# Splits, loads and norm steps around an MLP's products, put in another order

## The chip, the core and the metric

The kernel runs on one core of one Trainium2 chip. The time is device microseconds of one execution of the whole program on that core, and the figure that counts is the median over runs. In the views of the profile PE is TensorE (matmuls and transposes; PEld is its weight load), DVE is VectorE, ACT is ScalarE, POOL is GpSimd and SP is SyncE, which here only issues DMA transfers; POOL issues DMA transfers too. "L72" is line 72 of the kernel. Each engine works through its own instructions in a fixed order, and that order is settled when the program is built.

## The reference

A small decoder of two layers over 512 tokens and a width of 1024. Layer 0 mixes tokens by gated linear attention, layer 1 by stick-breaking attention; each is followed by a post-LayerNorm, an MLP of width 4096 and another post-LayerNorm:

```python
def layer_norm(x, g, b):
    xf = x.astype(jnp.float32)
    mu = jnp.mean(xf, axis=-1, keepdims=True)
    var = jnp.mean(jnp.square(xf - mu), axis=-1, keepdims=True)
    y = (xf - mu) * lax.rsqrt(var + LN_EPS)
    return (y * g.astype(jnp.float32) + b.astype(jnp.float32)).astype(x.dtype)

def sq_relu_mlp(x, w_up, w_down):
    h = jax.nn.relu(x @ w_up)
    return (h * h) @ w_down

    for layer in range(DEPTH):
        ...
        h = layer_norm(DEEPNORM_ALPHA * h + mix, ln_g[layer, 0], ln_b[layer, 0])
        h = layer_norm(DEEPNORM_ALPHA * h + sq_relu_mlp(h, mlp_w_up[layer], mlp_w_down[layer]),
                       ln_g[layer, 1], ln_b[layer, 1])
```

Everything is in fp32. After MLP 0 the shared keys and values (`kv_w`) and the queries of layer 1 are computed.

## The kernel before

**Products.** An fp32 product is made of three matmuls: each operand is split into a high part (`hi`, a copy to fp32r on ACT) and a low part (`lo`, the difference, on DVE), and hi x hi, hi x lo and lo x hi are summed in PSUM. A weight piece of 256 x 512 (a tile of 128 x 1024, half a megabyte) is split by `split_tile` (L70 on ACT, L72 on DVE); an operand made from activations is split by `put` (L98 on ACT, L99 on DVE). The split pieces lie in two pools, tags `hi` and `lo`, of eight buffers each; weights that are split straight after their load come through `raw`, three buffers (`split_piece`, L64).

**Seven steps.** A product of 2 x 2 blocks is done as seven block products instead of eight, by sums of blocks. In the output projection of layer 0 these are `seven` (L348 on): its last three products are called p3, p7 and p4, each of two halves s of 12 matmuls (L402), and each half is added to a row tile of the residual stream (`add`, L167 and L169 on DVE). In the MLP they are the seven steps of `steps` (L835): `make_blocks` loads and splits the weights of a step, `make_operand` sums and splits its activations, `go` runs its matmuls and reads the banks. Some block sums are done by DMA: `Blocks.more` (L761) adds a second block onto a loaded one by an accumulating load on POOL's queue, and `sum` (L784, L786) adds two loaded blocks, on POOL's DMA queue or on DVE.

**The MLP.** `mlp` (L806) takes the width of 4096 in four chunks c; each chunk has seven up steps (`part` at L942, matmuls L951, 48 of 256 columns each) and seven down steps (`part` at L992, matmuls L998, 24 of 512 columns). `todo` is the list of all 56 steps. `run_all` (L1022) writes them in order: at step n it prepares step n + 2. At step 0 it prepares steps 0, 1 and 2. The first two steps of chunk 0 take unsummed weights, four pieces of `plain` (L981 to L984): in MLP 0 they are loaded there, in MLP 1 they are handed over in `up0`, loaded and split inside `project` (L1483 to L1492).

**The joints.** Four row tiles t of 128 tokens are normed one after the other as their last additions come in. `finish` (L284) does it: `stats` (two DVE statistics L177, their sum L182, then `ve` L183 and the power `rs` L184 on POOL) and `centre` (L192 on DVE); then `turn_affine` transposes the centred tile in two halves (L271 on PE) and applies gain and bias in four copies per half (L274 on ACT). Tiles 0 and 1 are turned first (their second halves in `seconds`, pinned); tiles 2 and 3 are kept back in the list `late`, which the up step's `part` works off between matmuls. At the end of an MLP, tiles 0 and 1 get their statistics by sums on ACT (`stats_apart`, L206: a sum L209, `less` L210 on DVE, the squares L211, `ve` L212 on DVE, the power L213 on POOL). In MLP 0 this joint leads into `values` (L1090, matmuls L1111), in MLP 1 into the output (`done1`).

**What sets the order.** A list scheduler orders each engine's instructions by priority, which is their order in the program text, as soon as it reckons their inputs ready; statistics and centring are marked as urgent (`tc.high_priority`). `keep`, which is `tc.keep_in_program_order`, pins an instruction behind everything written before it on its engine. DMA issues are instructions of the queue's engine, SP or POOL, and stand in the same order.

## Time and profile before

| what | us |
|---|---|
| median of 3 runs | 1111.3 (1111.24 to 1111.48) |
| the profiled execution | 1109.4 |
| its span, first to last instruction | 1107.7 |
| PE busy | 1083.0 (98%) |
| DVE busy | 901.0 (81%) |
| ACT busy | 673.9 (61%) |
| POOL busy | 170.6 (15%) |

The profiled execution is one of its own, 1.9 us shorter than the median; what lies between its span and its time, 1.7 us, is before the first and after the last instruction of the program. PE is nearly always busy, so most of what the other engines do lies beside matmuls and costs nothing; a row of DVE or ACT matters where PE waits for it. The views give for a group or an instruction its duration and, in brackets, how long its engine stood idle before it and which instruction ended that idle time.

### The profile page before, as it was taken

How to read it: one execution, taken by the hardware profiler on the slowest of the kernel's cores; microseconds unless marked ns; L12 is line 12 of the kernel's file. 1: busy time of each engine (PE TensorE's matmuls, PEld its weight loads, DVE VectorE, ACT ScalarE, POOL GpSimd, SP SyncE). 2: the span in 40 equal slices, each digit the busy share in tenths (PEclk: the TensorE clock that was granted, in tenths of full speed). 3: DMA queues.
4: the chain of work that ended last, by engine and by line, in shares of the span. 5: the costliest groups of instructions: out<-in, count | busy, mean ns of one | idle time of the engine just before them, and what ended most of it. 6: DMA issues, size and time to landing. Idle time of an engine off the chain costs nothing. (4 is left out here: it accounts for less than half of the span.)

```text
span 1107.7 us, 16724 instructions
## 1 busy us (share of the span) xinstructions
PE 1083.0 (98%) x6463; PEld 936.9 (85%) x6463; DVE 901.0 (81%) x1086; ACT 673.9 (61%) x973; POOL 170.6 (15%) x201
## 2 busy tenths in 40 slices
PE   9999999989999999999999999999999999999997
PEld 7888888788899898898688778788888998988985
DVE  4488646989988978877888987689899889788778
ACT  4455436487557466465784766684875565574664
POOL 1021130302102101101203001222111021011012
PEclk9999999999999999999999999999999999999999
DMA  7262395688859949958837524478678598499583
GB/s 222 76 175 70 118 246 157 163 233 207 240 143 233 232 139 234 242 136 195 222 81 190 134 96 114 95 150 248 174 185 253 136 245 229 137 225 243 148 217 76
DMA packets 121891, 195.43 MB, mean 176 GB/s; under 512 B 13978, under 2 KB 38938, under 8 KB 121812
## 3 DMA queue, kind: packets, MB, share of 16 engines
q1 hardware_dynamic: 94932, 136.16, 38.4%
q0 software_dynamic: 26592, 57.68, 29.3%
q8 instruction: 51, 0.84, 0.3%
q10 hardware_dynamic: 288, 0.52, 0.1%
q14 instruction: 28, 0.23, 0.1%
HBM read 176.52 MB, written 3.15 MB: 162 GB/s over the span
## 5 line engine op out<-in xcount | busy, mean ns | idle before, releaser
L72 DVE TENSOR_TENSOR lo<-B,hi 128x1024 fp32r<-128x1024 f32 x206 | 246.7, 1220 | 60.7 <-ACT hi L70 58.6
L70 ACT ACTIVATE hi<-B 128x1024 fp32r<-128x1024 f32 x206 | 212.3, 1054 | 123.3 <-DVE B L786 63.4
L998 PE MATMUL ps<-hi,T 128*128 128x512 f32 x896 | 280.4, 391 | 1.8 <-DVE T L99 1.5
L951 PE MATMUL ps<-T,hi 128*128 128x256 f32 x1280 | 233.9, 284 | 6.3 <-ACT T L98 4.1
L951 PEld LDWEIGHTS ps<-T,hi 128*128 128x128 f32 x1280 | 200.1, 192 | 10.3 <-ACT T L98 4.9
L998 PEld LDWEIGHTS ps<-hi,T 128*128 128x128 f32 x896 | 167.6, 188 | 38.8 <-DVE T L99 3.4
L951 PE MATMUL ps<-T,lo 128*128 128x256 f32 x640 | 179.9, 283 | 0.0
L998 PE MATMUL ps<-lo,T 128*128 128x512 f32 x448 | 174.9, 390 | 2.8 <-DVE lo L72 2.8
L951 PEld LDWEIGHTS ps<-T,lo 128*128 128x128 f32 x640 | 122.3, 192 | 0.3
L72 DVE TENSOR_TENSOR lo<-raw,hi 128x1024 fp32r<-128x1024 f32 x86 | 103.0, 1216 | 20.1 <-ACT hi L70 19.7
L70 ACT ACTIVATE hi<-raw 128x1024 fp32r<-128x1024 f32 x88 | 91.0, 1056 | 38.7 <-PE ps L94 9.4
L998 PEld LDWEIGHTS ps<-lo,T 128*128 128x128 f32 x448 | 84.2, 188 | 20.8 <-DVE lo L72 4.0
L951 PE MATMUL ps<-A,hi 128*128 128x256 f32 x512 | 92.5, 283 | 0.0
L93 PE MATMUL ps<-T,hi 128*128 128x512 f32 (+1 forms) x200 | 79.7, 399 | 0.4 <-DVE k L99 0.4
L951 PEld LDWEIGHTS ps<-A,hi 128*128 128x128 f32 x512 | 79.9, 192 | 0.0
L98 ACT ACTIVATE T<-s 128x1024 fp32r<-128x1024 f32 (+1 forms) x52 | 51.5, 993 | 43.7 <-DVE s L883 37.6
L761 POOL DMA_DIRECT2D B<-in_mlp_w_down_dram x32 | 38.3, 1198 | 257.5 <-DMA B<-in_mlp_w_down_dram 126.0
L94 PE MATMUL ps<-T,hi 128*128 128x512 f32 (+1 forms) x200 | 76.5, 383 | 0.1
L95 PE MATMUL ps<-T,lo 128*128 128x512 f32 (+1 forms) x200 | 76.5, 383 | 0.0
L169 DVE TENSOR_TENSOR h<-h,ps 128x512 f32<-128x512 f32 x108 | 70.9, 678 | 2.8 <-PE ps L998 2.8
L951 PE MATMUL ps<-A,lo 128*128 128x256 f32 x256 | 72.4, 283 | 0.0
L99 DVE TENSOR_TENSOR T<-s,T 128x1024 fp32r<-128x1024 f32 (+1 forms) x52 | 59.2, 1138 | 5.7 <-ACT T L98 5.7
(239 smaller groups left out, 1877.6 us busy)
## 6 DMA issues: line engine op xcount, KB each, us to landing
B<-in_mlp_w_up_dram SPq DMA_DIRECT2D x64, 512.0 KB, 5.2
B<-in_mlp_w_down_dram SPq DMA_DIRECT2D x64, 512.0 KB, 4.9
B<-in_mlp_w_up_dram POOLq DMA_DIRECT2D x32, 512.0 KB, 8.3
B<-in_mlp_w_down_dram POOLq DMA_DIRECT2D x32, 512.0 KB, 9.4
raw<-in_mlp_w_up_dram SPq DMA_DIRECT2D x24, 512.0 KB, 4.6
B<-B POOLq DMA_DIRECT2D x24, 512.0 KB, 5.8
raw<-in_gla_w_in_dram SPq DMA_DIRECT2D x20, 512.0 KB, 3.7
raw<-in_mlp_w_down_dram SPq DMA_DIRECT2D x16, 512.0 KB, 8.2
```

What stands on the lines that cost most here:

```text
L70: keep(nc.scalar.activation(hi, raw, AF.Copy))
L72: keep((on or nc.vector).tensor_tensor(lo, raw, hi.bitcast(F32), op=ALU.subtract))
L93: keep(nc.tensor.matmul(ps, lhsT=a[0], rhs=b[0], start=first, stop=False))
L94: keep(nc.tensor.matmul(ps, lhsT=a[0], rhs=b[1], start=False, stop=False))
L95: keep(nc.tensor.matmul(ps, lhsT=a[1], rhs=b[0], start=False, stop=last))
L98: keep(nc.scalar.activation(hi, ps, AF.Copy))
L99: keep((on or nc.vector).tensor_tensor(lo, ps, hi.bitcast(F32), op=ALU.subtract))
L169: nc.vector.tensor_tensor(h, h, ps, op=op)
L761: keep(nc.gpsimd.dma_start(out=got[h].rearrange("p (a b) -> p a b", a=2), in_=self.w(other[0], h, other[1]), accum_op=ALU.add))
L951: nc.tensor.matmul(to, lhsT=b[k][x][:, fs], rhs=a(k)[:, y], start=opens and f % 2 == 0 and (k, x, y) == (0, 0, LO), stop=closes and (k, x) ...
L998: nc.tensor.matmul(banks[s], lhsT=a(k)[:, x][:, P * s:P * s + P], rhs=b[k][y], start=opens and (k, x, y) == (0, LO, 0), stop=closes and (k ...
```

## The change

It adds and removes no matmul. Its parts, in the order of the kernel:

- In `seven`, the splits of p4 are written after the second addition of p3, pinned on ACT and DVE.
- In MLP 0, pieces 1 and 2 of the first weights are loaded through POOL's queue and not pinned; piece 3 stays pinned on SP. The accumulating loads onto block (1, 1) are issued by `late`, after a small POOL copy that reads tile 3's `rs` and pins them behind it.
- In both MLPs, the blocks of step 2 are written after the matmuls of step 0; tile 3 is turned in step 0 and no longer in step 1; steps 8 to 13 make their operand before their blocks; the matmuls of the first down step are pinned.
- In `project`, the last piece of the first weights of MLP 1 is loaded and split after the last addition, unpinned.
- `stats_apart` is cut in two. Tiles 0 and 1 both draw their sums first, then both their squares; `less` and `ve` are computed on ACT.

```diff
-    def split_piece(src, a, turn=lambda ins: ins, **how):
+    def split_piece(src, a, turn=lambda ins: ins, queue=nc.sync, **how):
...
-        turn(nc.sync.dma_start(out=raw.rearrange("p (a b) -> p a b", a=a), in_=src))
+        turn(queue.dma_start(out=raw.rearrange("p (a b) -> p a b", a=a), in_=src))
...
-            total, less, squares, ve, rs = (small(1, tag) for tag in ("total", "less", "squares", "ve", "rs"))
+            self.junk = junk
+            total, self.less = small(1, "total"), small(1, "less")
             nc.scalar.activation(junk, self.h, AF.Copy, accum_out=total)
-            nc.vector.tensor_scalar(less, total, -1.0 / D, None, op0=ALU.mult)
-            nc.scalar.activation(junk, self.h, AF.Square, bias=less, accum_out=squares)
-            nc.vector.tensor_scalar(ve, squares, 1.0 / D, LN_EPS, op0=ALU.mult, op1=ALU.add)
-            nc.gpsimd.tensor_tensor(rs, ve, mhalf[:, 0:1], op=ALU.pow)
-            self.less, self.rs = less, rs
+            nc.scalar.activation(self.less, total, AF.Copy, scale=-1.0 / D)
+
+        def power_apart(self):
+
+            squares, ve, self.rs = small(1, "squares"), small(1, "ve"), small(1, "rs")
+            nc.scalar.activation(self.junk, self.h, AF.Square, bias=self.less, accum_out=squares)
+            nc.scalar.activation(ve, squares, AF.Copy, scale=1.0 / D, bias=LN_EPS)
+            nc.gpsimd.tensor_tensor(self.rs, ve, mhalf[:, 0:1], op=ALU.pow)
...
                     hs[t].stats_apart(junk)
+                    if t == 1:
+                        for h in hs[:2]:
+                            h.power_apart()
+                            h.centre()
                 else:
                     hs[t].stats()
-                hs[t].centre()
+                    hs[t].centre()
...
-        p4 = split_a(a22), split_b(3)
         for s in range(2):
             part(s, *p3, zs, False, True)
             add(s, zs, 0, 1, last=True)
+            if s == 1:
+                p4 = split_a(a22, keep=tc.keep_in_program_order), split_b(3, keep=tc.keep_in_program_order)
             yield s
...
-                made.append(Blocks(mlp_, weights, AHEAD[2:] + AHEAD[:1], by))
+                made.append(Blocks(mlp_, weights, (AHEAD[2], (1, 1, None if late_sum else (0, 1)), AHEAD[0]), by))
...
+                    me.late = lambda: [made[0].more(made[0].b[1, 1], (0, 1), h, keep) for h in range(2)]
...
-                    if c == 0 and late and (n == 0 and m == 9 and len(late) > 1 or n == 1 and m == 1):
+                    if c == 0 and n == 0 and late and m in (9, 13):
                         late.pop(0)()
...
-                    plain = [piece(0)] + [lambda k=k: piece(k, turn=keep) for k in (1, 2, 3)]
-                made = steps(r[0], r[2], r[1], r[3], w, part, read, ((1, 0),), plain, ops, (6,))
+                    plain = [piece(0)] + [lambda k=k: piece(k, queue=nc.gpsimd) for k in (1, 2)] + [lambda: piece(3, turn=keep)]
+                made = steps(r[0], r[2], r[1], r[3], w, part, read, ((1, 0),), plain, ops, (6,), late_sum=l == 0)
...
+                            if c == n == 0:
+                                keep(ins)
...
-                for m in range(n, n + 3) if n == 0 else (n + 2,) if n > 5 and not last else ():
+                for m in range(n, n + 2) if n == 0 else (n + 2,) if n > 5 and not last else ():
                     if m < len(todo):
+                        if 7 < m < 14:
+                            todo[m].make_operand()
                         todo[m].make_blocks()
-                        if m > 6 or m < 2:
+                        if m < 2 or m > 13:
                             todo[m].make_operand()
                         if m == 0:
                             late.pop(0)()
+                            if l == 0:
+                                keep(nc.gpsimd.tensor_copy(out=small(1, "pin"), in_=hs[3].rs))
+                                todo[3].late()
...
                     if n == 0:
+                        todo[2].make_blocks()
                         todo[3].sums()
...
-        up0.extend(pieces_512(mlp_w_up[1], 512, 4, 0, keep=keep))
+        up0.extend(pieces_512(mlp_w_up[1], 512, 2, 0, keep=keep))
         run(STEPS[4:], whole(256), b4, us, False)
         add(1, us, 1, 0, last=True)
         yield 3
+        up0.extend(pieces_512(mlp_w_up[1], 768, 2, 0))
...
                 hs[t].stats_apart(work()[:, 0:D])
+                if t == 1:
+                    for h in hs[:2]:
+                        h.power_apart()
```

More of the change, by code (lines that the diff above doesn't have):

```diff
@@ L334, in yoco_kernel, with split_a @@
     A0, A1 = slice(0, 64), slice(64, P)
-    def split_a(a):
+    def split_a(a, **how):
         u = unit(F32R)
-        put(u[:, :, 0:256], u[:, :, 256:512], a)
+        put(u[:, :, 0:256], u[:, :, 256:512], a, **how)
         return lambda k, s: (u[:, k, 128 * s:128 * s + 128], u[:, k, 256 + 128 * s:384 + 128 * s])
@@ L747, in __init__, with load @@
             self.load(order)
-        def load(self, order, start=lambda **to: nc.sync.dma_start(**to)):
+        def load(self, order):
             for k, j, other in order:
@@ L753, in load @@
                     b = self.pool.tile([P, 1024], F32, tag="B", bufs=8, name=nm("B"))
-                    start(out=b.rearrange("p (a b) -> p a b", a=2), in_=self.w(k, h, j))
+                    nc.sync.dma_start(out=b.rearrange("p (a b) -> p a b", a=2), in_=self.w(k, h, j))
                     got.append(b)
@@ L833, in views, with steps @@
             return lambda k: us[k // n][:, k % n, :]
-        def steps(a11, a12, a21, a22, weights, part, read, by=(), plain=None, ops=None, held=(), last=False):
+        def steps(a11, a12, a21, a22, weights, part, read, by=(), plain=None, ops=None, held=(), last=False, late_sum=False):
             made, t = [], []
@@ L997, in part @@
                         for x, y in ((LO, 0), (LO, 1), (HI, 0)):
-                            nc.tensor.matmul(banks[s], lhsT=a(k)[:, x][:, P * s:P * s + P], rhs=b[k][y],
-                                             start=opens and (k, x, y) == (0, LO, 0),
-                                             stop=closes and (k, x) == (3, HI), skip_group_check=True)
+                            ins = nc.tensor.matmul(banks[s], lhsT=a(k)[:, x][:, P * s:P * s + P], rhs=b[k][y],
+                                                   start=opens and (k, x, y) == (0, LO, 0),
+                                                   stop=closes and (k, x) == (3, HI), skip_group_check=True)
+                            if c == n == 0:
+                                keep(ins)
                     yield s
```

## The prediction

> **What bounds the kernel now.** I read the page's head, then TensorE's busy time by stretch, then its waits in the stretches that are not full.
>
> ```profile
> span 1107.7 us, 16724 instructions
> ```
>
> ```profile
> 197.00:236.00 39.00, 33.77 (x202) 1.00 0.73 189
> 236.00:290.00 54.00, 52.15 (x340) 1.00 0.86 216
> 290.00:518.00 228.00, 228.00 (x1479) 1.00 0.78 198
> 518.00:549.00 31.00, 28.09 (x124) 0.99 0.75 200
> ...
> 760.00:792.00 32.00, 28.85 (x188) 1.00 0.72 218
> 792.00:842.00 50.00, 48.04 (x321) 1.00 0.83 207
> ```
>
> (Stretch, its length, PE busy, clock, DMA share, GB/s.) PE has no hole in the 228 us of MLP 0's later chunks, so the products set the time there, and the change adds no matmul. What can be won is idle time at the joints: 5.23 us from 197 to 236 (attention output into MLP 0), 1.85 in MLP 0's first chunk, 2.91 where MLP 0 meets the values' product, 3.15 and 1.96 at the two places of MLP 1 that answer to the first two, and the tail.
>
> **Place A, head of MLP 0.** PE's longest waits from 205 to 236, then rows of ACT, DVE, POOL and SP, each in order of time:
>
> ```profile
> PE ps L951 <- ACT T L98: 3.1, 2, 1.7
> PE ps L951 <- DVE T L99: 0.8, 1, 0.8
> ```
>
> ```profile
> 210.09 1.51 ACT L274 ACTIVATE T<-ps,bcol,gcol 128x128 f32<-128x128 f32 x4 [12.71 <-PE ps L271]
> ...
> 217.66 1.16 ACT L274 ACTIVATE T<-ps,bcol,gcol 128x128 f32<-128x128 f32 x3 [1.74 <-PE ps L271]
> 218.70 1.07 ACT L70 ACTIVATE hi<-raw 128x1024 fp32r<-128x1024 f32 x1
> ...
> 225.33 2.06 ACT L70 ACTIVATE hi<-B 128x1024 fp32r<-128x1024 f32 x2
> 227.22 4.71 ACT L274 ACTIVATE T<-ps,bcol,gcol 128x128 f32<-128x128 f32 x13
> ```
>
> ```profile
> 201.44 1.22 DVE L99 TENSOR_TENSOR T<-T,T 128x1024 fp32r<-128x1024 f32 x1
> 202.57 2.35 DVE L72 TENSOR_TENSOR lo<-B,hi 128x1024 fp32r<-128x1024 f32 x2
> 204.84 1.28 DVE L169 TENSOR_TENSOR h<-h,ps 128x512 f32<-128x512 f32 x2
> ...
> 219.22 0.81 DVE L192 TENSOR_SCALAR h<-h,mv,rs 128x1024 f32<-128x1024 f32 x1 [1.00 <-POOL rs L184]
> ```
>
> ```profile
> 209.62 1.56 POOL L761 DMA_DIRECT2D B<-in_mlp_w_up_dram  x1
> 210.40 1.64 POOL L184 TENSOR_TENSOR rs<-ve,mhalf 128x1 f32<-128x1 f32 x1
> ```
>
> ```profile
> 196.15 15.84 SPq L64 DMA_DIRECT2D raw<-in_mlp_w_up_dram  x3
> ```
>
> ACT stands idle for 12.71 us before 210 and for 1.74 before 217.66, waits there for the turning of tile 2, and only then splits piece 1 (218.70), whose load is the first of the three issued from 196 on. From there to 231.9 it is dense, with the other pieces, block splits and affine copies in one queue, and PE waits for the ends of that queue (3.1 + 0.8). Four edits act here.
>
> First, `p4`'s splits, three DVE instructions (201.44 to 204.84, 3.4 us), move behind row tile 1's last addition. The pair of additions at 204.84 no longer queues behind them, so tiles 0 and 1 are centred about 3 us earlier. The splits still have to be ready when p4's products begin; the 24 matmuls of p7, 5.5 us, are their cover, and without it PE would wait up to 3.4 us. Second, two accumulating loads go behind the last `rs`, pinned, which takes their POOL issues (1.56) from in front of an `rs` like that of 210.40. Behind the pin nothing but those loads is queued soon on POOL; DVE's sum waits for them, eight us and more before step 3 uses it. Third, pieces 1 and 2 load through POOL's queue, two more issues of about 1.56 us where POOL has nothing to do, and their splits, 2.1 us of ACT, should fall into ACT's hole. SP's queue loses two pinned waits for a buffer. Fourth, `todo[2].make_blocks()` comes after step 0's products, so the 2.06 us at 225.33 no longer stand before the last 13 copies; tile 3 is turned 12 matmuls sooner.
>
> What a plain load on POOL takes no row shows; bounds are the page's landing times of SP's plain loads and POOL's accumulating ones:
>
> ```profile
> B<-in_mlp_w_up_dram POOLq DMA_DIRECT2D x32, 512.0 KB, 8.3
> raw<-in_mlp_w_up_dram SPq DMA_DIRECT2D x24, 512.0 KB, 4.6
> ```
>
> I take 8.3, the nearer in its queue: both pieces are there by 208, eight us before step 0 needs the first. The Trainium skill ("DMA: Bandwidth & Descriptors", section Issuing engines are not separate DMA queues) says that transfers from all issuing engines run on the same 16 engines, so that another queue saves the time of the issue alone. By that rule the move wins nothing by itself; the first rival below is worked out from rows for that case.
>
> **Place A goes on** in the first chunk, where matmuls of the first down step (L998) are issued ahead of the last up step (L951) and wait there:
>
> ```profile
> 260.20 0.50 PE L998 MATMUL ps<-lo,T 128*128 128x512 f32 x1 [1.08 <-DVE lo L72]
> ...
> 262.14 0.40 PE L951 MATMUL ps<-T,hi 128*128 128x256 f32 x2
> ```
>
> ```profile
> 283.81 0.73 PE L998 MATMUL ps<-hi,T 128*128 128x512 f32 x2 [0.77 <-DVE T L99]
> ```
>
> The pin on those matmuls sends PE straight into the up step, which started without a wait at 262.14: 1.08 go. Operands before blocks, in steps 8 to 13, aim at the 0.77. But DVE limits the sum of all this (its busy time, by stretch):
>
> ```profile
> 206.00:290.00 84.00, 77.75 (x88) 1.00 0.85 214
> 760.00:842.00 82.00, 75.61 (x85) 1.00 0.79 212
> ```
>
> If DVE ran at 97% of the time, an estimate between these 93% and a full queue, 77.75 us of work would take 80.1: the stretch can shrink by 3.9 us, though PE idles for 3.9 + 1.85 in it. Tile 3's norm chain, which no edit touches, keeps most of its wait of 1.00. **A = 3.2**; bounds 0 and 5.7, PE's whole idle time.
>
> **Place B, MLP 0 into the values.**
>
> ```profile
> 536.27 1.15 ACT L211 ACTIVATE junk<-h,less 128x1024 f32<-128x1024 f32 x1 [2.08 <-DVE less L210]
> 537.33 0.18 ACT L211 ACTIVATION_READ_ACCUMULATOR junk<-h,less 128x1 f32 x1
> ```
>
> ```profile
> PE ps L1111 <- DVE T L99: 1.8, 1, 1.8
> ...
> PE ps L271 <- DVE h L192: 0.3, 1, 0.3
> PE ps L1111 <- ACT T L98: 0.2, 1, 0.2
> ```
>
> ```profile
> 546.00:548.40 2.40, 0.65 (x4) 1.00 1.02 186
> 548.40:551.90 3.50, 3.50 (x10) 0.51 1.06 255
> ```
>
> ACT waits 2.08 us for a small instruction with which DVE is late. Now `less` and `ve` are ACT's own, four instructions more. No 128x1 ACTIVATE is in the trace. The bounds are the 0.18 of reading an accumulator and 0.38, a quarter of the four 128x128 copies at 210.09; I take 0.2, as the width is that of the first, so 0.8 in all. Against it stands the 2.08: tile 1's sum is drawn before tile 0's squares, tile 1 is centred about 2 us earlier, and the two pinned pieces behind it with it. Next late is the `lo` half of tile 0's turned rows, behind those pieces' splits on DVE: of the 1.8 + 0.2 about 0.6 stay, and the 0.3 goes; that is 1.7. PE's hole, 0.65 busy of 2.40 us, is followed by 3.5 us at a granted clock of 0.51, which cost 3.5 x 0.49 = 1.7 more. The two waits of place A, the longer 1.7, left the clock at 1.00 in the row from 197, so a wait of 0.6 should too: 1.7 more, less 0.2 for safety. The Trainium skill ("TensorE: Matmul & The Clock Gate", Part 1) lets the clock fall to half after an idle window of about 3.4 us. Here it fell after a shorter one; by the rule alone a hole of this size costs no clock, and B would be 1.5. **B = 3.2**; bounds 0 and 4.0.
>
> **Place C, MLP 1.** DVE's order before tile 3's last addition, and PE's waits from 760 to 792:
>
> ```profile
> 776.90 1.22 DVE L72 TENSOR_TENSOR lo<-raw,hi 128x1024 fp32r<-128x1024 f32 x1
> 778.03 0.68 DVE L169 TENSOR_TENSOR h<-h,ps 128x512 f32<-128x512 f32 x1
> ```
>
> ```profile
> PE ps L951 <- DVE T L99: 1.4, 3, 0.8
> PE ps L951 <- ACT T L98: 1.0, 1, 1.0
> PE ps L271 <- DVE h L192: 0.8, 1, 0.8
> ```
>
> The last piece's split stands pinned in front of tile 3's addition. It moves behind it: the addition comes at least 1.1 us earlier, and PE's 0.8 for `h` goes. The 1.0 behind it shrinks by about 0.6, as the block splits leave the copies' way here too. The pin and the operand order could win the 1.96 of the first chunk; PE then comes to step 10 sooner than DVE, and I keep 0.6. **C = 2.0**; bounds 0 and 4.1 (75.61 us at 97% is 77.9 of 82).
>
> **Tail.** Four small DVE instructions leave DVE here as well. I estimate 0.05 each, a quarter of the 0.18 of the smallest row above, since neighbours on a queue overlap: **0.2**, bounds 0 and 0.7.
>
> **Sum.** 3.2 + 3.2 + 2.0 + 0.2 = 8.6. The span becomes 1099.1, the profiled execution (1109.4) 1100.8; the median of the runs stands 1.9 above that execution, so **1102.7**.
>
> **Rivals.** *The queue changes nothing* (chance 0.18): the order on ACT is the scheduler's, piece 1's split stays behind tile 2's copies, and the hole of 12.71 us stays. For it: the load was issued at 196 already, and the hole was there. A shrinks to the pin's 1.0; total 6.4, 1104.9. *DVE takes it back* (0.18): PE reaches the down steps sooner, DVE does not, and the waits of L998 grow. For it stands DVE's 93%; against it, that part of its waits goes with PE's. A 1.5, C 0.5, with B and tail 5.4: 1105.9. *Only the pins act* (0.13): the scheduler permutes the rest at no gain. 1.08 twice, less 0.8 given back at step 10, is 1.4: 1109.9. *Slower* (0.09): operands before blocks puts every block split one L72 or L99 (1.13 from start to start at 201.44) later in steps 8 to 13 of both MLPs, and PE waits for `lo` in each: 12 x 1.13 = 13.6, added to my forecast 1116.3. It decides from 8.6/12 = 0.72 us a step. Against it: these steps are prepared two ahead, so one late split need not be waited for.
>
> **Chances and range.** My forecast has 0.42. A measurement of this kernel tells a change of over 0.2%, 2.2 us, from none. The forecast and the first two rivals are faster, 0.78; the pins alone are the same, 0.13; slower 0.09. The range, 1098.0 to 1110.0, takes in all but the slower case and the outermost ends: with all upper bounds (5.7 + 4.0 + 4.1 + 0.7) it would be 1096.8.
>
> **What would show it.** Right: L70 on `raw` before 210, in the hole; PE's waits from 205 to 236 under 2 us; no L998 before the last L951 of the first chunk; L211 without a wait for DVE, and no clock of 0.5 near 550; L169 ahead of the last L72 near 777. Wrong: new waits of L402 (p4 too late), of L951 for the late accumulating loads, or of L998 for `lo` in steps 8 to 13.

## The result and the profile after

The change made the kernel slower: 1126.0 us (median of 4 runs, 1121.3 to 1127.5) against 1111.4 beside it, a ratio of 1.0122 with a 95% interval of 1.0090 to 1.0154. The forecast was 1102.7, the range 1098.0 to 1110.0. The profiled execution took 1121.3 us, the shortest of the four, so the views below account for 11.9 of the 14.6 us. Its page begins (span; PE's busy time, instructions):

```profile
span 1119.6 us, 16733 instructions
...
PE 1083.8 (97%) x6463; PEld 941.9 (84%) x6463; DVE 900.0 (80%) x1078; ACT 675.5 (60%) x981; POOL 170.8 (15%) x204
```

The span grew by 11.9 us and PE's busy time by 0.8 (it was 1083.0): nearly all of the profiled loss is PE standing idle (35.8 us instead of 24.7). Busy time by stretch of the changed kernel, in the columns start:end, length, PE, PEld, DVE, ACT, POOL, granted clock, DMA share, GB/s:

```profile
197.00:236.00 39.00, 32.94 (x203) 28.50 (x201) 31.63 (x41) 24.03 (x48) 11.95 (x16) 0.98 0.71 187
236.00:290.00 54.00, 47.55 (x305) 44.78 (x306) 47.88 (x49) 34.46 (x40) 6.57 (x6) 0.89 0.71 179
290.00:518.00 228.00, 228.00 (x1479) 209.09 (x1478) 188.44 (x190) 137.20 (x150) 33.35 (x29) 1.00 0.79 199
760.00:792.00 32.00, 29.92 (x177) 26.05 (x176) 25.07 (x35) 19.08 (x42) 5.56 (x9) 1.00 0.83 241
792.00:842.00 50.00, 42.66 (x306) 40.88 (x305) 44.76 (x45) 35.51 (x44) 6.62 (x6) 0.93 0.68 167
```

The loss lies in the two heads and first chunks: from 197 to 290 PE idles 12.5 us instead of 7.1, from 760 to 842 9.4 instead of 5.1, and the clock is under 1.00 in both. DVE, which was busy for 52.14 of 54 us from 236 to 290, is now busy for 47.88: the engine that bounded this stretch stands idle too. PE's longest waits there, MLP 0 (205 to 290) and then MLP 1 (760 to 850); the lines have moved, L961 is the up step's matmul (L951 before), L978 DVE's reading of its banks (L968), L1008 the down step's (L998), L410 the projection's (L402), L275 a transpose (L271); further down L877 is `tmp` (L868), L795 a pinned sum (L786) and L278 ACT's affine copy (L274):

```profile
PE ps L961 <- DVE T L99: 4.8, 1, 4.8
PE ps L961 <- DVE s L978: 4.3, 1, 4.3
PE ps L410 <- DVE h L169: 1.2, 1, 1.2
```

```profile
PE ps L961 <- DVE s L978: 4.6, 1, 4.6
PE ps L961 <- DVE T L99: 3.0, 2, 2.6
```

Two waits account for most of it in each MLP: one at the start of step 2, for the `lo` half of its operand (4.8 and 2.6 us), and one ahead of the last up step, step 6, for DVE's reading of two banks (4.3 and 4.6). Half clock sets in during three of these four waits and lasts 6.8 us each time. Each place has its own mechanism.

**Step 2.** DVE's rows in order of time, before and after (start, duration, instruction, in brackets the idle time ahead of it and what ended it):

```profile
226.75 2.35 DVE L72 TENSOR_TENSOR lo<-B,hi 128x1024 fp32r<-128x1024 f32 x2
229.02 2.35 DVE L786 TENSOR_TENSOR B<-B,B 128x1024 f32<-128x1024 f32 x2
231.96 1.23 DVE L868 TENSOR_TENSOR tmp<-T,T 128x1024 f32<-128x1024 f32 x1 [0.59 <-ACT T L274]
233.10 1.28 DVE L968 TENSOR_TENSOR s<-s,ps 128x512 f32<-128x512 f32 x2
234.31 1.23 DVE L99 TENSOR_TENSOR T<-tmp,T 128x1024 fp32r<-128x1024 f32 x1
```

```profile
229.01 1.22 DVE L877 TENSOR_TENSOR tmp<-T,T 128x1024 f32<-128x1024 f32 x1 [1.21 <-ACT T L278]
230.16 2.35 DVE L72 TENSOR_TENSOR lo<-B,hi 128x1024 fp32r<-128x1024 f32 x2
232.43 1.22 DVE L795 TENSOR_TENSOR B<-B,B 128x1024 f32<-128x1024 f32 x1
235.71 1.23 DVE L795 TENSOR_TENSOR B<-B,B 128x1024 f32<-128x1024 f32 x1 [2.06 <-DMA B<-in_mlp_w_up_dram]
236.85 1.22 DVE L99 TENSOR_TENSOR T<-tmp,T 128x1024 fp32r<-128x1024 f32 x1
```

Before, DVE did the two block splits of step 2 (L72) and the two pinned sums (L786) while ACT still made the last copies; then came `tmp`, the sum for step 2's operand, and 2.35 us after its start the operand's `lo` (L99). After, ACT's copies are done earlier, as forecast, and `tmp` starts at 229.01, 2.95 us sooner. But the four instructions that had filled the waiting time now stand between `tmp` and L99, and the second sum waits 2.06 us for a late accumulating load. L99 comes 7.84 us after `tmp`, 2.5 us later than before.

**Step 6** accumulates into the two banks that step 5 has just filled, so it may start only when DVE has drawn step 5's result from the first of them; it also needs the `hi` half of its operand from ACT. In the kernel before, DVE's two readings and ACT's copy stand at

```profile
261.20 1.27 DVE L968 TENSOR_TENSOR s<-s,ps 128x512 f32<-128x512 f32 x2
```

```profile
260.90 1.06 ACT L98 ACTIVATE T<-s 128x1024 fp32r<-128x1024 f32 x1
```

so that step 6 could not start before 261.96, when the copy is over and the first reading just has been. Before, PE ran ten matmuls of the first down step in that time, eight of them between the prediction's rows of 260.20 and 262.14. Pinned, they stand behind step 6.

### The profile page after: what moved, and what is told of

It is laid out like the page before. It is cut to its first block, busy times and chain, and to the rows that moved or that the text cites. A ratio compares the mean times of both kernels' runs of the same rounds, so it can differ in the third digit from the quotient of the medians.

```text
span 1119.6 us, 16733 instructions
## 1 busy us (share of the span) xinstructions
PE 1083.8 (97%) x6463; PEld 941.9 (84%) x6463; DVE 900.0 (80%) x1078; ACT 675.5 (60%) x981; POOL 170.8 (15%) x204
## 5 line engine op out<-in xcount | busy, mean ns | idle before, releaser
L72 DVE TENSOR_TENSOR lo<-B,hi 128x1024 fp32r<-128x1024 f32 x206 | 246.8, 1219 | 66.4 <-ACT hi L70 63.9
L70 ACT ACTIVATE hi<-B 128x1024 fp32r<-128x1024 f32 x206 | 212.1, 1054 | 131.6 <-DVE B L795 63.5
L1008 PE MATMUL ps<-hi,T 128*128 128x512 f32 x896 | 279.7, 390 | 0.3 <-DVE h L169 0.2
L961 PE MATMUL ps<-T,hi 128*128 128x256 f32 x1280 | 238.7, 288 | 17.3 <-DVE s L978 8.9
L961 PEld LDWEIGHTS ps<-T,hi 128*128 128x128 f32 x1280 | 204.7, 196 | 20.5 <-ACT T L98 10.3
L1008 PEld LDWEIGHTS ps<-hi,T 128*128 128x128 f32 x896 | 167.9, 188 | 36.4 <-DVE h L169 0.8
L961 PE MATMUL ps<-T,lo 128*128 128x256 f32 x640 | 182.5, 287 | 0.0
L1008 PE MATMUL ps<-lo,T 128*128 128x512 f32 x448 | 174.6, 390 | 0.7 <-DVE lo L72 0.7
L961 PEld LDWEIGHTS ps<-T,lo 128*128 128x128 f32 x640 | 125.1, 196 | 0.2
L72 DVE TENSOR_TENSOR lo<-raw,hi 128x1024 fp32r<-128x1024 f32 x86 | 102.7, 1217 | 17.4 <-ACT hi L70 17.0
L70 ACT ACTIVATE hi<-raw 128x1024 fp32r<-128x1024 f32 x88 | 90.8, 1055 | 41.2 <-PE ps L94 10.6
L1008 PEld LDWEIGHTS ps<-lo,T 128*128 128x128 f32 x448 | 84.2, 188 | 18.0 <-DVE lo L72 1.1
L961 PE MATMUL ps<-A,hi 128*128 128x256 f32 x512 | 92.5, 283 | 0.0
L961 PEld LDWEIGHTS ps<-A,hi 128*128 128x128 f32 x512 | 79.9, 192 | 0.0
L169 DVE TENSOR_TENSOR h<-h,ps 128x512 f32<-128x512 f32 x108 | 70.9, 678 | 2.0 <-PE ps L1008 1.8
L961 PE MATMUL ps<-A,lo 128*128 128x256 f32 x256 | 72.4, 283 | 0.0
L99 DVE TENSOR_TENSOR T<-s,T 128x1024 fp32r<-128x1024 f32 (+1 forms) x52 | 59.1, 1136 | 7.2 <-ACT T L98 7.2
```

What stands on the lines that cost most here:

```text
L70: keep(nc.scalar.activation(hi, raw, AF.Copy))
L72: keep((on or nc.vector).tensor_tensor(lo, raw, hi.bitcast(F32), op=ALU.subtract))
L99: keep((on or nc.vector).tensor_tensor(lo, ps, hi.bitcast(F32), op=ALU.subtract))
L169: nc.vector.tensor_tensor(h, h, ps, op=op)
L961: nc.tensor.matmul(to, lhsT=b[k][x][:, fs], rhs=a(k)[:, y], start=opens and f % 2 == 0 and (k, x, y) == (0, 0, LO), stop=closes and (k, x) ...
L1008: ins = nc.tensor.matmul(banks[s], lhsT=a(k)[:, x][:, P * s:P * s + P], rhs=b[k][y], start=opens and (k, x, y) == (0, LO, 0), stop=closes ...
```

## The experiments

Each kernel was timed beside the kernel before. Medians and ratios:

| kernel | us (runs) | ratio, 95% interval |
|---|---|---|
| changed kernel | 1126.0 (4) | 1.0122, 1.0090 to 1.0154 |
| e1 pin alone | 1116.7 (5) | 1.0042, 1.0026 to 1.0058 |
| e2 change without pin | 1124.8 (4) | 1.0110, 1.0095 to 1.0126 |
| e3 e2, blocks back | 1119.4 (4) | 1.0054, 1.0038 to 1.0071 |
| e4 e3, no late loads | 1115.3 (6) | 1.0029, 1.0018 to 1.0041 |
| e5 statistics alone | 1113.1 (12) | 1.0006, 0.9992 to 1.0020 |
| e6 pieces and p4 alone | 1112.0 (11) | 0.9991, 0.9980 to 1.0001 |
| e7 operand first alone | 1113.8 (12) | 1.0011, 0.9995 to 1.0027 |
| e8 turns alone | 1113.1 (12) | 1.0002, 0.9988 to 1.0017 |
| e9 change, blocks back | 1123.4 (4) | 1.0087, 1.0057 to 1.0117 |
| e10 change, sums later | 1123.3 (4) | 1.0087, 1.0060 to 1.0114 |
| e11 pieces alone | 1109.6 (12) | 0.9969, 0.9952 to 0.9987 |
| e12 e11 and ACT's small values | 1109.7 (12) | 0.9969, 0.9953 to 0.9985 |
| e13 late loads alone | 1111.6 (10) | 0.9987, 0.9973 to 1.0000 |
| e14 e4 with moved blocks | 1123.0 (4) | 1.0093, 1.0073 to 1.0113 |
| e15 e11 and the tail | 1110.0 (11) | 0.9964, 0.9948 to 0.9981 |
| e16 e15, sums later | 1111.7 (12) | 0.9994, 0.9977 to 1.0012 |
| e17 e3, p4 back | 1116.2 (10) | 1.0037, 1.0022 to 1.0052 |
| e18 e15 and late loads | 1114.8 (12) | 1.0024, 1.0011 to 1.0036 |

The kernel before had a median of 1111.4 beside the changed kernel and of 1112.0 to 1112.8 beside the others.

### The pin: e1 and e2

e1 is the kernel before with the pin; e2 is the changed kernel without it.

```diff
+                            if c == n == 0:
+                                keep(ins)
```

> The kernel before, with the one edit that pins the matmuls of the first down step. Theory 1 (those matmuls were cover: the seventh up step must wait until DVE has drawn the fifth step's result from the banks that both use, and pinned they no longer fill that wait): PE waits 4 to 5 us for L978 in the first chunk of each MLP and runs at half clock for some us behind it; 8 to 11 us slower than before, near 1120. Theory 2 (the loss lies in DVE's queue at step 2, the pin is harmless): same as before or 1 to 2 us faster, 1109 to 1112.

> The changed kernel without that pin. Theory 1: no wait for L978 over 1.5 us and no half clock near 265 and 825; 8 to 11 us faster than the changed kernel, 1114 to 1118, since the wait of step 2 (4.8 and 2.6 us, half clock near 234) stays. Theory 2: within 2 us of the changed kernel, 1122 to 1127.

e1 was 4.5 us slower than the kernel before. PE's start of step 6 and DVE's reading of step 5's banks in e1, then the stretch behind it in the columns of the busy times:

```profile
262.30 0.55 PE L951 MATMUL ps<-T,hi 128*128 128x256 f32 x1 [3.38 <-ACT T L98]
```

```profile
261.47 1.27 DVE L968 TENSOR_TENSOR s<-s,ps 128x512 f32<-128x512 f32 x2
```

```profile
261.40:268.20 6.80, 5.91 (x28) 5.93 (x29) 4.75 (x6) 3.56 (x4) 1.72 (x2) 0.50 1.11 208
```

Step 6 starts at 262.30; before, it started at 262.14. The pin brought it nothing, since the wait belongs to the banks (the first of the two readings at 261.47 has to be over) and to the operand: the profile puts the wait down to ACT's copy, which ended about 0.1 us behind that reading, and no run separates the two. What the pin did was empty the wait: 3.38 us idle instead of 1.08, and half clock for 6.8 us around its end. So theory 1 has the mechanism, with half the size that it gave. Taking the pin out of the changed kernel, though, won only 1.2 us, which is within the spread, so there the time came out as theory 2 had it. DVE was late in any case: the wait ahead of step 2 stayed (the first line below), and in place of the 4.3 us ahead of step 6 the first of the matmuls set free waited 2.0 us for a block's `lo` (the second line; e2, 205 to 295):

```profile
PE ps L961 <- DVE T L99: 5.7, 1, 5.7
PE ps L1008 <- DVE lo L72: 3.1, 2, 2.0
```

### The blocks of step 2: e3, e9, e14 and e10

e3 is e2, and e9 the changed kernel, with step 2's blocks where they were:

```diff
-                for m in range(n, n + 2) if n == 0 else (n + 2,) if n > 5 and not last else ():
+                for m in range(n, n + 3) if n == 0 else (n + 2,) if n > 5 and not last else ():
...
-                        todo[2].make_blocks()
```

> The changed kernel without the pin, and with step 2's blocks made before step 0's products again, ahead of the pinned sums; the late accumulating loads stay. If it is the sums ahead of step 2's lo operand on DVE that make the wait of 4.8 us (theory 2), it goes, with the half clock behind it, in both MLPs: 5 to 8 us faster than the kernel without the pin alone, 1107 to 1112. If the late loads hold step 2 by another way, the wait in MLP 0 stays over 2 us and only MLP 1 gains: 1112 to 1116.

> The changed kernel with step 2's blocks made before step 0's products again; the pin and the late loads stay. If parts add up: 5 to 6 us faster than the changed kernel (as without the pin, 1124.8 to 1119.4), near 1120.5, the wait of 4.3 us for L978 still there. If DVE's queue is one limit that pin, moved blocks and late loads press on together, the pin's wait covers part of it and the sum's 3.6 us of waiting for the late loads stays: 2 to 4 us faster, 1122 to 1124.

e3 won 5.4 us over e2, e9 only 2.6 over the changed kernel, whose four runs are spread over 6 us. Of the two readings of e9 the second has the size: DVE's sums still waited 3.7 us for the late loads, and PE 3.4 us ahead of step 6 in each MLP (put down to ACT's operand, as in e1).

e14 is the changed kernel without the pin and without the late loads, which is e4 (below) with the moved blocks.

> The changed kernel without the pin and without the late loads: of its three costly edits only the moved blocks of step 2 are left. If the moved blocks cost by themselves (two splits and two sums ahead of step 2's lo operand on DVE, whatever the sums wait for): 2 to 4 us slower than the kernel without all three (1115.3), 1117 to 1119.5, with a wait of over 2 us ahead of step 2 in both MLPs. If they cost only through the sums' wait for the late loads: MLP 1 alone pays, under 1.5 us slower, 1115 to 1117.

1123.0 against e4's 1115.3: the moved blocks cost 7.7 us by themselves (7.1 by the ratios), twice what the higher theory gave. DVE's rows in e14, then the same `tmp` and `lo` in e4:

```profile
230.80 1.23 DVE L877 TENSOR_TENSOR tmp<-T,T 128x1024 f32<-128x1024 f32 x1 [3.65 <-ACT T L278]
231.94 2.35 DVE L72 TENSOR_TENSOR lo<-B,hi 128x1024 fp32r<-128x1024 f32 x2
234.21 2.36 DVE L795 TENSOR_TENSOR B<-B,B 128x1024 f32<-128x1024 f32 x2
236.48 1.22 DVE L99 TENSOR_TENSOR T<-tmp,T 128x1024 fp32r<-128x1024 f32 x1
```

```profile
233.05 1.22 DVE L877 TENSOR_TENSOR tmp<-T,T 128x1024 f32<-128x1024 f32 x1 [1.02 <-ACT T L278]
235.40 1.23 DVE L99 TENSOR_TENSOR T<-tmp,T 128x1024 fp32r<-128x1024 f32 x1
```

No sum waits for a load here. DVE stands idle for 3.65 us until ACT has made the copies, and only then does the 4.5 us of work that used to lie in that hole, ahead of the L99 for which PE waits. `tmp` comes 2.25 us sooner than in e4 and the `lo` 1.08 us later. So PE gets to step 2 sooner and waits there: 5.6 and 2.9 us in all at its start in the two MLPs, 3.9 and 1.8 in e4. The delay goes on from there, as 2.0 us of waiting for a block's `lo` in the first down step of each MLP (none and 1.1 in e4). In the two profiles, 7.7 us apart as well, PE idles 33.4 us instead of 29.1 and is busy for 1088.6 instead of 1085.2, at a mean clock of 0.990 instead of 0.994: part of the price is half clock.

e10 is the changed kernel with the pinned sums behind step 2's operand:

```diff
                     if n == 0:
                         todo[2].make_blocks()
-                        todo[3].sums()
                     if n == 1:
                         todo[0].read()
                         todo[2].make_operand()
+                        todo[3].sums()
                         todo[3].minus()
```

> The changed kernel, with one edit: DVE's pinned sums of step 3's blocks are issued after step 2's operand, behind step 0's read, instead of ahead of it. Theory 2 (the sums at the head of DVE's queue, waiting for the late loads, hold the lo operand of step 2): the wait of 4.8 us ahead of step 2 in MLP 0 falls under 2 us, that of 2.6 us in MLP 1 under 1.2, the half clock near 234 may go; 4 to 7 us faster than the changed kernel, 1119 to 1122. Rival (the moved block splits L72 alone hold it, or tile 3's norm): within 2 us of the changed kernel, with a wait of over 3 us there.

The waits ahead of step 2 fell as theory 2 said, from 4.8 to 0.9 us and from 2.6 to at most 0.4, and still only 2.7 us were won, which is within the spread of the changed kernel: in MLP 0 step 3 now waited 1.6 and 0.6 us for its blocks' `hi` and `lo`, and step 6 4.8 instead of 4.3. The same sums had still to be done ahead of step 3's splits: part of what was taken off one wait came back in the next two.

### The late loads: e4, e13, e17 and e18

e4 is e3 with the accumulating loads issued with their plain loads again; e13 is the kernel before with the late loads alone. Their edit (e13):

```diff
-                made.append(Blocks(mlp_, weights, AHEAD[2:] + AHEAD[:1], by))
+                made.append(Blocks(mlp_, weights, (AHEAD[2], (1, 1, None if late_sum else (0, 1)), AHEAD[0]), by))
...
+                            if l == 0:
+                                keep(nc.gpsimd.tensor_copy(out=small(1, "pin"), in_=hs[3].rs))
+                                todo[3].late()
```

> As the kernel with step 2's blocks back and no pin, and without the two late accumulating loads (they are issued with their plain loads again). If the late loads cost nothing once step 2's blocks stand ahead of the sums: within 1.5 us of that kernel, on either side. If DVE's sum still waits for them (it waited 2.06 us in the changed kernel) and step 3 or 4 is late by it: 1.5 to 4 us faster. If they win what was meant (POOL's rs not behind two issues of 0.8 us each): 1 to 2 us slower.

> The kernel before, with only the two accumulating loads of step 3's block in MLP 0 issued late, behind the last rs on POOL. Theory L (DVE, the bound of the first chunk, stands still in its pinned sums until the loads land, about 3.6 us of idle DVE in all, and step 1's or 2's lo operand behind them): 2.5 to 5 us slower than before, 1114.5 to 1117, DVE's idle time from 204 to 292 about 10 us instead of 6.2. Rival (the prediction: the sum has eight us of slack): same within 1 us.

e4 was 4.0 us faster than e3, so the loads cost there; alone (e13) they cost nothing, against theory L. To see why, e17 puts p4's splits back in e3, and e18 adds the late loads to e15 (below), which has the pieces on POOL's queue and p4's splits where they were:

```diff
+        p4 = split_a(a22), split_b(3)
         for s in range(2):
             part(s, *p3, zs, False, True)
             add(s, zs, 0, 1, last=True)
-            if s == 1:
-                p4 = split_a(a22, keep=tc.keep_in_program_order), split_b(3, keep=tc.keep_in_program_order)
```

> The kernel without the pin and with step 2's blocks back (1119.4; late loads and all else of the change kept), with one more edit undone: p4's splits stand before row tile 1's last addition again. Theory D (the late loads cost nothing alone; they cost 4 us there because the moved splits make p4's products, tile 3's rs and so the pinned loads later by 2 to 3 us): the loads are issued near 221 instead of 223.6, DVE's idle time in front of the two sums falls from 3.6 us to under 1, PE's wait of 6.0 us ahead of step 1's last matmuls under 3.5; 3.5 to 6 us faster than that kernel, 1113.5 to 1116. Rival (the loads are slow by themselves, 8 to 10 us from issue to landing, wherever rs stands): within 2 us of it, 1117.5 to 1121.

> The kernel with the pieces on POOL's queue and the tail's statistics (1110.0), with the late loads added, p4's splits, step 2's blocks and the matmuls left as before. Theory D: the sums wait under 0.5 us, as with the late loads alone: 1109 to 1111, below the kernel before. Rival: the pieces make the block splits earlier, so that the sums meet loads that have not landed: 1.5 us of idle DVE or more, 1112 to 1115.

Theory D, that the moved p4 makes the loads late, fell. e17 won 3.1 us, between the two forecasts, but its sums still wait 4.3 us for the loads (3.6 in e3). And e18, with p4 as before, is 4.8 us slower than e15. PE's wait ahead of step 2 is 6.9 us in e18, for the `hi` that ACT makes from `tmp`, and 1.1 in e15. DVE's rows of e13 and of e18 (L800 is the pinned sum):

```profile
228.01 2.36 DVE L72 TENSOR_TENSOR lo<-B,hi 128x1024 fp32r<-128x1024 f32 x2
230.28 2.36 DVE L786 TENSOR_TENSOR B<-B,B 128x1024 f32<-128x1024 f32 x2
```

```profile
224.20 2.35 DVE L72 TENSOR_TENSOR lo<-B,hi 128x1024 fp32r<-128x1024 f32 x2
228.30 1.22 DVE L800 TENSOR_TENSOR B<-B,B 128x1024 f32<-128x1024 f32 x1 [1.75 <-DMA B<-in_mlp_w_up_dram]
233.34 1.22 DVE L800 TENSOR_TENSOR B<-B,B 128x1024 f32<-128x1024 f32 x1 [3.81 <-DMA B<-in_mlp_w_up_dram]
```

In e13 the block splits start at 228.01 and the sums behind them meet loads that have landed. With the pieces split early the block splits start at 224.20, and DVE stands 5.6 us in its pinned sums, with `tmp` behind them. Of the 5.6 us, 3.8 are DVE's coming sooner. The rest is the loads' own: issued at 222.00 instead of 220.76, the second lands about 10.5 us after its issue instead of 9.5 or less, at 233.34, so even sums at e13's pace, the second at 231.4, would have come nearly 2 us too soon for it. The late loads are free only as long as something else makes DVE late enough. e17 lacks e3's wait of 1.2 us at p4's products, and its longest wait is 0.9 shorter (5.1 instead of 6.0 us); where the rest of its 3.1 us came from is left open.

### The small parts: e5, e6, e7 and e8

e5 is the kernel before with `stats_apart` cut in two, as in the diff of the change, and its two calls, of which the one at MLP 0's end is shown:

```diff
                     hs[t].stats_apart(junk)
+                    if t == 1:
+                        for h in hs[:2]:
+                            h.power_apart()
+                            h.centre()
```

e6 has p4's splits behind the addition (the diff of e17, the other way round) and the pieces on POOL's queue (that of e11, below). e7 has the order of operand and blocks:

```diff
+                        if 7 < m < 14:
+                            todo[m].make_operand()
                         todo[m].make_blocks()
-                        if m > 6 or m < 2:
+                        if m < 2 or m > 13:
                             todo[m].make_operand()
```

e8 has the turns:

```diff
-                    if c == 0 and late and (n == 0 and m == 9 and len(late) > 1 or n == 1 and m == 1):
+                    if c == 0 and n == 0 and late and m in (9, 13):
...
-        up0.extend(pieces_512(mlp_w_up[1], 512, 4, 0, keep=keep))
+        up0.extend(pieces_512(mlp_w_up[1], 512, 2, 0, keep=keep))
...
+        up0.extend(pieces_512(mlp_w_up[1], 768, 2, 0))
```

> The kernel before, with only the split of the two-tile statistics (both sums first, then both squares, ACT making the small values itself). Theory S (the prediction's term B and tail, 3.2 + 0.2): no wait of ACT for DVE, no half clock where MLP 0 meets the values, 3.4 us faster, about 1108. Theory S' (read from the changed kernel: the wait only moves, from the turned rows' lo half to tile 0's centring, since the turns stand earlier in PE's order; PE waits 2.1 us there and 1.4 us near the values' end, but keeps its full clock, and the tail gains 0.9): 1.5 to 2.5 us faster, 1109 to 1110.5.

> The kernel before, with only the two edits at the head of MLP 0 that are left in the kernel without the late loads: p4's splits behind row tile 1's last addition, and pieces 1 and 2 loaded through POOL's queue. Theory H (the prediction's term A without the pin, 3.2 less 1.1): about 2 us faster, 1110. Theory H' (a gain of 2 us up to step 0, given back in one wait of 3.4 us ahead of step 1 or 2 for the last of ACT's copies, with half clock behind it): 0 to 1.5 us slower, 1112 to 1113.5.

> The kernel before, with only the order of operand and blocks turned round in steps 8 to 13. Theory O (the prediction: the 0.77 us of waiting for the operand's lo half go in both MLPs): 0.5 to 1.5 us faster, 1110.5 to 1111.5. Theory O' (read from the kernels without the pin, which wait 1.04 us for the block's lo there and lose 1.2 us between there and chunk 1): 1 to 2.5 us slower, 1113 to 1114.5. The prediction's slower rival: 13.6 us slower.

> The kernel before, with only the two edits on turns: the project's last piece split in two, its second half behind row tile 3's last addition, and both late tiles turned within step 0 (at its matmul groups 9 and 13). Theory C (the prediction: 0.8 + 0.6 in MLP 1, 12 matmuls sooner in MLP 0): 1 to 2 us faster, 1110 to 1111. Theory C' (read from the changed kernel: tile 3's turn stands earlier in PE's order than its rows are ready, PE waits 1.7 us for them in MLP 1 instead of 0.8, and half clock may follow): 0.5 to 3 us slower, 1112.5 to 1115.

None of the four can be told from no change. What each moved is seen in PE's waits. e5 from 518 to 570 has, in place of the 1.8 for `lo` and the 0.3 for `h`:

```profile
PE ps L275 <- DVE h L192: 2.3, 1, 2.3
PE ps L94 <- DVE T L99: 1.4, 1, 1.4
```

ACT no longer waits for `less`, but tile 0 is centred after tile 1's sum, its transposes stand earlier in PE's order, and PE waits for them: the wait moved to `h`. Theory S fell, and S' was too high as well. e6 from 205 to 236, beside e11, which has the pieces without p4:

```profile
PE ps L953 <- ACT T L98: 3.8, 1, 3.8
PE ps L402 <- DVE h L169: 1.2, 1, 1.2
```

```profile
PE ps L951 <- ACT T L98: 1.7, 1, 1.7
PE ps L951 <- DVE T L99: 1.0, 2, 0.8
```

The moved splits make PE wait 1.2 us at p4's products, and with the end of those products comes tile 3's last addition, from which the rest of the head hangs. Theory H' has the place and size of the wait at step 2, 3.8 us where it gave 3.4; the whole is nearer to no change than either theory. In e7 PE waits 1.0 us for a block's `lo` where it had waited 0.77 for the operand's: the mechanism is that of O', while the interval reaches from 0.5 us faster to 3.0 slower. e8 from 760 to 796:

```profile
PE ps L271 <- DVE h L192: 1.7, 1, 1.7
```

The wait for `h` doubled, as C' said; the whole stayed the same, which neither theory had.

### What beats the kernel before: e11, e12, e15 and e16

e11 keeps one edit of the change:

```diff
-                    plain = [piece(0)] + [lambda k=k: piece(k, turn=keep) for k in (1, 2, 3)]
+                    plain = [piece(0)] + [lambda k=k: piece(k, queue=nc.gpsimd) for k in (1, 2)] + [lambda: piece(3, turn=keep)]
```

> The kernel before, with only pieces 1 and 2 of MLP 0's first blocks loaded through POOL's queue. Theory P (p4's moved splits delayed p4's products by 1.1 us, and with them tile 3's norm, on which the head hangs; the pieces alone fill ACT's hole of 12.7 us and let tile 3's copies come earlier): PE's waits from 205 to 236 fall from 4.9 to 2.5 to 4 us, no wait of L402 for h; 1 to 2 us faster than before. Rival (the wait is set by tile 3's norm chain alone, the hole costs nothing): same within 0.5 us, waits of 4.4 to 5 us there.

> As the kernel with the pieces alone, and with ACT making the small values itself; at the tail both tiles' sums come first as in the changed kernel, where MLP 0 meets the values each tile's statistics stay whole (sum, squares, centring, then the next tile). Theory: the tail gains 0.9 us (1.84 to 0.96 of waiting), and where MLP 0 meets the values the wait of ACT for DVE goes without the turns standing ahead of their rows: 0 to 1 us; in all 1 to 2 us faster than the pieces alone. Rival: the turns move ahead as in the kernel with the split statistics, waits of 2.3 and 1.4 us there, and the gain at the tail is given back: same as the pieces alone within 0.5 us.

> The kernel before with pieces 1 and 2 on POOL's queue, and the split statistics with ACT's small values at the tail alone; MLP 0 into the values stays as before. If the tail's 0.9 us is real and the split's cost where MLP 0 meets the values was what cancelled it: 0.9 us faster than the pieces alone (1109.6), 1108 to 1109.3. Rival: nothing is added, 1109.3 to 1110.3.

> As that, and with DVE's pinned sums of step 3's blocks issued behind step 2's operand. If they stand in the way of the lo operand here too (0.76 us of waiting ahead of step 2 in both MLPs): 0.5 to 1.5 us faster still, 1107 to 1108.5. Rival: step 3's block splits are then late (0.6 to 1.6 us of waiting ahead of step 3, as in the changed kernel with the sums later): same or up to 2 us slower, 1109 to 1111.

e11 is 3.1 us faster than the kernel before; its interval leaves out no change. PE's waits from 205 to 236 add up to 2.7 us, and PE is busy for 28.06 of these 31 us instead of 26.32. e12 added ACT's small values with each tile's statistics left whole at MLP 0's end, e15 the split at the tail alone, with the two halves of `stats_apart` named `sum_apart` and `power_apart`:

```diff
-                hs[t].stats_apart(work()[:, 0:D])
+                hs[t].sum_apart(work()[:, 0:D])
+                if t == 1:
+                    for h in hs[:2]:
+                        h.power_apart()
```

In the tail the wait fell from 1.8 to 1.0 us in e15's profile, but neither median shows it beside e11's; e12's turns went ahead again, as its rival said. e16, e15 with the sums behind step 2's operand (the edit of e10), cannot be told from the kernel before: in the first down step its profile has a wait of 2.0 us for a block's `lo` in each MLP, where the kernel before has 1.1 and 1.2; but e15 has 1.5 and 1.9 there, so this wait alone does not explain the 1.7 us between their medians. e11 is the version to keep: e12 and e15 add edits to it and no gain that shows.

## Why the prediction was wrong

Built up from e11, the ratios are 0.9969 (pieces), 0.9991 (and p4), 1.0029 (and statistics, turns, operand order), 1.0093 (and moved blocks), 1.0110 (and late loads), 1.0122 (and the pin). On 1112 us that is -3.4, +2.4, +4.2, +7.1, +1.9 and +1.3. Each step is uncertain by about 2 us, the last by 4, so the first, the third and the fourth are sure by themselves, and another order gives other shares: the pin costs 4.5 us alone, the late loads nothing. By place, in PE's idle time of the two profiles: A was forecast to win 3.2 us and lost 5.4 (197 to 290), C to win 2.0 and lost 4.3 (760 to 842).

- **The step that failed most** was "`todo[2].make_blocks()` comes after step 0's products, so the 2.06 us at 225.33 no longer stand before the last 13 copies". That is right for ACT. The same call issues two splits on DVE, with the pinned sums behind them, and there they had filled a wait. They cost 7.7 us (e14 against e4). The prediction counted the ACT instructions of the move and put the DVE ones at nothing.
- **The pin**: "sends PE straight into the up step, which started without a wait at 262.14: 1.08 go". The step started without a wait because other matmuls had covered it; its start was set by DVE's reading at 261.20 and ACT's copy at 260.90. e1: 4.5 us slower. What the row without a wait showed was a cover and not a slack.
- **Late loads**: "DVE's sum waits for them, eight us and more before step 3 uses it". The use of the sum was not the limit; its place in DVE's queue was. The slack is there alone (e13) and gone as soon as the pieces come early (e18: 5.6 us of standing still, 4.8 us slower than e15).
- **Pieces on POOL's queue**: right. L70 stands in ACT's hole, in the changed kernel at

```profile
201.30 1.06 ACT L70 ACTIVATE hi<-raw 128x1024 fp32r<-128x1024 f32 x1 [1.17 <-DMA raw<-in_mlp_w_up_dram]
204.87 1.06 ACT L70 ACTIVATE hi<-raw 128x1024 fp32r<-128x1024 f32 x1 [2.50 <-DMA raw<-in_mlp_w_up_dram]
```

and the edit alone won 3.1 us, so the rival that the queue changes nothing fell. The gain isn't in the transfer. From issue to landing the loads between 195 and 205 took, before on SP and in e11 on POOL:

```profile
raw<-in_mlp_w_up_dram SPq DMA_DIRECT2D x2, 512.0 KB, 3.6
```

```profile
raw<-in_mlp_w_up_dram POOLq DMA_DIRECT2D x2, 512.0 KB, 4.2
```

Off the pinned queue the splits stand in ACT's order ahead of the tiles' copies. The Trainium skill ("DMA: Bandwidth & Descriptors", section Issuing engines are not separate DMA queues) says that another queue saves the time of the issue alone; for the transfers these two rows agree with it. The prediction took 8.3 us for a load on POOL, from the accumulating ones; 4.2 was the size.

- **p4**: "the 24 matmuls of p7, 5.5 us, are their cover" looked at the wrong limit. p4's products accumulate into the banks that p7's have filled, so PE waits for the addition that draws the first of them, and this addition had queued behind p4's splits on DVE. In the changed kernel, DVE and then PE:

```profile
209.25 2.35 DVE L72 TENSOR_TENSOR lo<-B,hi 128x1024 fp32r<-128x1024 f32 x2
211.53 0.68 DVE L169 TENSOR_TENSOR h<-h,ps 128x512 f32<-128x512 f32 x1
```

```profile
212.35 0.47 PE L410 MATMUL ps<-hi,T 128*128 128x512 f32 x1 [1.17 <-DVE h L169]
```

The splits are over at 211.60 and the addition at 212.21. The delay runs on into tile 3.

- **Place B**: the forecast of 3.2 was wrong in both terms. The 2.08 of ACT went (the small values take ACT 0.20 us each in the changed kernel, as forecast) and came back as PE's wait for `h` (e5). The 1.7 for the clock was no property of the kernel: the same wait is followed by half clock in some profiles and not in others, and its absence here in the changed kernel's profile does not bear the term out: in e9, which has the same edit, the 3.4 us from 549.8 run at 0.52. PE's wait for `lo` here is 1.8 us in e6 and e11 alike (PE busy for 0.65 and 0.62 of the first 2.4 us); first e6, then e11, wait and what follows it:

```profile
548.20:550.60 2.40, 0.65 (x3) 0.56 (x4) 2.12 (x4) 2.40 (x8) 0.24 (x1) 1.00 0.95 169
550.60:554.00 3.40, 3.40 (x18) 2.79 (x17) 2.37 (x5) 3.40 (x8) 1.89 (x4) 1.00 1.09 266
```

```profile
546.80:549.20 2.40, 0.62 (x4) 0.53 (x4) 2.08 (x4) 2.40 (x8) 0.28 (x1) 1.00 1.01 182
549.20:552.60 3.40, 3.40 (x10) 2.63 (x9) 2.37 (x5) 3.40 (x8) 1.85 (x4) 0.50 1.07 266
```

- **Place C and the operand order**: the addition of tile 3 does come ahead of the last split, and nothing was won (e8, e7).
- **Tail**: 0.2 us forecast; the wait is 0.9 us shorter, and no median shows it.
- **The slower rival** had the right sign and the wrong mechanism: operands before blocks come to 1.2 us (e7), which cannot be told from none, not to 13.6.
- **The sum**: the prediction said that "DVE limits the sum of all this", gave 93%, and used it as a bound on the gain, with DVE fuller than before. DVE's busy time from 206 to 290 went from 77.75 us to 71.30 instead. The limit was not used for the price of what the edits add to DVE's queue or take away as its filling, which is where the time went.
- **The signs**: L70 in the hole, no L998 ahead of the last up step, no wait of L211 for DVE and L169 ahead of the last L72 all came, in a slower kernel: each told that a move had been made, none what it cost. PE's waits from 205 to 236, to be under 2 us, were 2.9, and the sign against p4 came too.

## What to carry to other kernels

When a step is moved, list its instructions on every engine, and for each ask what it filled where it stood: on an engine that bounds the stretch, work that lies in a wait is free there and can cost its full length, or more, anywhere else. A wait that a row doesn't show may be covered by the work in front of it, so ask what the next instruction would have waited for if that work were gone. Prices of such edits don't add up: here the same late loads cost nothing or 4.8 us, by how early the engine came to them and how late they landed, so test parts alone and together.

## What the hardware showed unasked

Between the start and the end of the program, spells of half clock lasted about 3.4 or 6.8 us in every profile of this study. At the joint of MLP 0 and the values ten profiles have a wait of 1.75 to 1.78 us for the turned rows; six of them show half clock behind it and four do not. In the changed kernel half clock set in during the waits of 4.8 and 4.3 us in MLP 0 and of 4.6 us in MLP 1 and lasted 6.8 us each time. The Trainium skill ("TensorE: Matmul & The Clock Gate", Part 1) describes a window of about 3.4 us that runs freely and an idle window that halves the clock; the lengths and the chance agree with it, while a wait of half a window was enough here. No run shows what share of a window must be idle.
